# A seven-product output projection: where the first weight sums are formed, which raw weights are kept, and the order of sums in the feed-forward's second round

## The chip, the cores and the metric

The kernel runs on one core of a Trainium2 chip. The metric is the device time in microseconds (us): the median of three runs, and beside it one profiled execution, in which every instruction has a start, a duration and the line of the kernel that issued it.

The engines have the names of the profile: PE (TensorE, matmuls), PEld (its weight loads), DVE (VectorE), ACT (ScalarE), POOL (GpSimd) and SP (SyncE, which here only issues loads). Each engine runs its instructions in the order in which the compiler put them.

## The reference

One decoder layer over x of 512 rows and 1024 columns, all in float32: three gated branches, an output projection `w_o`, and a SwiGLU feed-forward.

```python
merged = g[:, :, 0] * y_a + g[:, :, 1] * y_b + g[:, :, 2] * y_c
x = x + merged @ w_o[l]

hf = rms_norm(x, ffn_norm_g[l]) @ w_ffn_in[l]
gt, up = jnp.split(hf, 2, axis=-1)
x = x + (jax.nn.silu(gt) * up) @ w_ffn_out[l]
```

`y_a` is an attention branch, `y_b` a convolution branch with a layer norm (it is the last one computed), `y_c` a short convolution.

## The kernel before

**Numbers.** Each float32 operand is split in two: `hi` is a rounded copy (fp32r, made by ScalarE, line 81), `lo` the rest (`src - hi`, by VectorE, line 82). A product of two operands is three matmuls: hi·hi, hi·lo, lo·hi (`mm3`, line 90 issues every matmul).

**Seven products.** `merged @ w_o` and the two halves of the second feed-forward matrix (12 and 10 row blocks, `ffn_out`) are done by Strassen's scheme in Winograd's form. The contraction goes over *pairs* of row blocks of 128: four pairs in `w_o`, six and five in the feed-forward halves. For a pair, the activations are cut in four quarters (`quarters`, lines 559 to 562 form four sums of quarters, then everything is split), and so is the weight: b11, b12, b21, b22, each 128 rows by 512 columns. The seven products 1 to 7 use, on the weight's side, b11, b21, b22, t2 - b21 (product 4), t1 = b12 - b11 (product 5), t2 = b22 - b12 + b11 (product 6) and t3 = b22 - b12 (product 7). In the feed-forward the operand of product 4 is formed afresh as t4. `seventh` does one product of one pair: two banks of PSUM, three matmuls each, six matmuls.

**Three rounds of the output projection.** Eight banks do not hold all results at once, so the products are done in rounds over the pairs:

- Round one: products 1, 6, 7 of all pairs. For each pair j, `raw3` loads b11, b12, b22 in three loads of 256 KB into one "raw" buffer; lines 811 and 812 form t3 and t2; `parts` splits b11 and `parts2` splits t2 and t3, both into "wh" and "wl" buffers. PE's order is (pair, product): (0,1), (1,1), (0,6), (0,7), (2,1), (1,6), (1,7), (3,1), (2,6), (2,7), (3,6), (3,7).
- `middle` (lines 614 to 623) joins the three results: copies by ScalarE, line 615 adds, line 620 makes the start value of product 4's banks (the returned `change`), and line 623 adds to two blocks of x1.
- Round two: products 2 and 4 of each pair. Line 827 loads all four b21 in one load of 1 MB; line 830 subtracts it from t2. Then lines 836 and 838 add to x1 (the last of these is `half`).
- Round three: products 5 and 3. `raw3` loads b11, b12, b22 once more for each pair, line 845 forms t1, `parts2` splits b22 and t1. PE's order is (0,5), (0,3), (1,5), a turn, (1,3), a turn, (2,5), (3,5), a turn, (2,3), a turn, (3,3). A turn (line 773) transposes a block of the finished x1 for the feed-forward; lines 777 and 778 scale and split it, line 783 squares it.

**Feed-forward.** `ffn_in` computes the two input products; `ffn_out` does round one (1, 6, 7) and then a round with 2, 3, 5 and 4: for pair j, `parts` splits b21 and b22 (from the raw weights), lines 934 to 936 form t1 and t4 in a "tt" buffer, and `parts` splits these. PE does (j,2), (j,3), then (j-1,5), (j-1,4). In the last half the last two pairs are regrouped, product by product.

**What sets the order.** PE's order is the program's own (a manual schedule). On the other engines a scheduler orders the instructions at compile time: by program order, with `tc.high_priority()` moving work ahead, `tc.issue_after(i)` keeping work behind instruction i, and each instruction waiting until its buffer is free. Buffers have tags, each with a fixed count: "raw" 3 (a load's target), "wh" and "wl" 3 (split weights), "t" 6 (temporaries, `tmp()`), "c" 4, "u" 16 (the normalised input of the branches, and later that of the feed-forward), "tt" 2, "l2" 1.

**Around it.** The branches are a queue of units, each one block of 128 output columns. The last branch has 16: a gate unit (24 matmuls) and a product unit (12) for each of eight blocks. Its last product unit ends with lines 650 and 651 and the last `quarters`. `drain()` empties the queue, and the output projection's code comes after it.

Of the kernel before, what the change touches and what calls it, by code (L numbers as in the profile page):

```python
# [9 lines left out]
F32R = mybir.dt.float32r  # L10
# [4 lines left out]
P = 128  # L15
S = 512
D = 1024
KT = D // P
# [17 lines left out]
def hybrid_layer(ctx, tc, x, mix_norm_g, w_in, q_norm_g, k_norm_g, w_attn_out, conf_dw_w,  # L36
# [23 lines left out]
    def alloc(tag, shape=(P, S), dt=F32):  # L60
        count[0] += 1
        where = ps if tag in ("mm", "z", "o") else odd if tag in ("c", "cf") else sb
        return where.tile(list(shape), dt, tag=tag, name=f"{tag}_{count[0]}", bufs=BUFS[tag])

    def psum(tag="mm"):
        return alloc(tag)

    def tmp(dt=F32, shape=(P, S)):
        return alloc("t", shape, dt)
# [533 lines left out]
    def x1_at(i, c):  # L603
        return x1[c][:, i, :]

    def middle(p1, p6, p7):


        p5 = [psum(tag) for tag in ("z", "o")]
        s2, s7 = [tmp(), tmp()], []  # L610
        with tc.high_priority(offset=PRIO):
            for i in range(2):
                s1 = tmp()
                nc.scalar.copy(s1, p1[i])
                nc.vector.tensor_add(s2[i], p6[i], s1)
                nc.scalar.copy(p5[i], s2[i])
            for i in range(2):
                s7.append(tmp())
                nc.scalar.copy(s7[i], p7[i])
                change = nc.vector.scalar_tensor_tensor(p7[i], p7[i], -1.0, s2[i], ALU.mult,  # L620
                                                        ALU.subtract)
        for i in range(2):
            nc.vector.tensor_add(x1_at(i + 2, 1), s7[i], x1_at(i + 2, 1))
        return p5, change.ins


    merged = {}
# [127 lines left out]

    bra = list(branch(0, w_attn_out, lambda: oT))
    queue += bra[:8] + [call(conf_mean_start)] + bra[8:]
    queue += branch(1, w_conf_out, lambda: hb, last=True)
    drain()


# [24 lines left out]
        return square  # L786

    n = KT // 2
    wo_q = lambda j, k, c: w_o[(2 * j + k) * P:(2 * j + k + 1) * P, c * S:(c + 1) * S]

    def raw3(j):
        with tc.high_priority():
            w = alloc("raw", (P, 3, S))
            for i, (k, c) in enumerate(((0, 0), (0, 1), (1, 1))):
                nc.sync.dma_start(w[:, i], wo_q(j, k, c))
        return [w[:, i] for i in range(3)]

    p1, p6, p7 = [[psum(tag) for _ in range(2)] for tag in ("mm", "mm", "z")]
    def after(*ins):
        stack = ExitStack()  # L800
        stack.enter_context(tc.high_priority())
        for i in ins:
            stack.enter_context(tc.issue_after(i))
        return stack

    t2s, last_sum, todo = [], [], []
    for j in range(n):
        b11, b12, b22 = raw3(j)
        with after(*last_sum):
            t3, t2 = tmp(), alloc("c")  # L810
            nc.vector.tensor_sub(t3, b22, b12)  # L811
            last_sum = [nc.vector.tensor_add(t2, t3, b11).ins]
        t2s.append(t2)
        one, = parts(b11.rearrange("p (n f) -> p n f", n=1))
        two = parts2(t2, t3)

        todo += [(j, 1, one, p1), (j, 6, two[0], p6), (j, 7, two[1], p7)]
        order = [0] if j == 0 else [2, 0, 1] if j < n - 1 else [2, 0, 1, 3, 4]
        for k in order:
            i, p, w, banks = todo[k]  # L820
            seventh(mT[i][p], w, banks, i == 0)
        todo = todo[1:] if j == 0 else todo[3:]
    p5, change = middle(p1, p6, p7)

    with tc.high_priority():
        b21 = alloc("raw", (P, n, S))
        nc.sync.dma_start(b21, w_o[:, :S].rearrange("(j k p) f -> p j k f", p=P, k=2)[:, :, 1])
    for j in range(n):
        with after(*[change][:j]):
            nc.vector.tensor_sub(t2s[j], t2s[j], b21[:, j])  # L830
        two, four = parts2(b21[:, j], t2s[j])
        seventh(mT[j][2], two, p1, False)
        seventh(mT[j][4], four, p7, False)
    with tc.high_priority(offset=PRIO):
# [4 lines left out]
    p3 = [psum("mm") for _ in range(2)]  # L839
    held = []  # L840
    for j in range(n):
        b11, b12, b22 = raw3(j)
        with after(*[half][:j]):
            t1 = tmp()
            nc.vector.tensor_sub(t1, b12, b11)
        held.append(parts2(b22, t1))
        if j == n - 2:
            continue
        for p in (5, 3):
            for i in range(j, j + 1) if j < n - 2 else (n - 2, n - 1):  # L850
                seventh(mT[i][p], held[i][p // 4], p5 if p == 5 else p3, i == 0 and p == 3)

                if j == 1 or j == n - 1 and (i, p) in ((n - 1, 5), (n - 2, 3)):
                    turn(len(u2))()
# [46 lines left out]
    def ffn_out(j0, h, last):  # L901
        n = len(h)
        rows_of = lambda j, k: w_ffn_out[(j0 + 2 * j + k) * P:(j0 + 2 * j + k + 1) * P]


        p1, p6, p7 = [[psum(tag) for _ in range(2)] for tag in ("mm", "mm", "z")]
        for j in range(n):
            with tc.high_priority():
                w = alloc("raw", (P, 3, S))
                nc.sync.dma_start(w[:, 0:2], rows_of(j, 0).rearrange("p (n f) -> p n f", n=2))  # L910
                nc.sync.dma_start(w[:, 2], rows_of(j, 1)[:, S:])
            b11, b12, b22 = [w[:, i] for i in range(3)]

            def t32(t3, t2):
                nc.vector.tensor_sub(t3, b22, b12)
                nc.vector.tensor_add(t2, t3, b11)

            one, = parts(w[:, 0:1])
            t3, t2 = parts(sums(t32))
            for p, w, banks in ((1, one, p1), (6, t2, p6), (7, t3, p7)):  # L920
                seventh(h[j][p], w, banks, j == 0)
        p5, change = middle(p1, p6, p7)
        p3, p4 = [psum("mm") for _ in range(2)], p7
        products = lambda j, p, w, banks, start: seventh(h[j][p], w, banks, start and j == 0)
        todo, behind, formed = [], [], []
        for j in range(n):
            with tc.high_priority():
                w = alloc("raw", (P, 2, 2, S))
                nc.sync.dma_start(w, w_ffn_out[(j0 + 2 * j) * P:(j0 + 2 * j + 2) * P].rearrange(
                    "(k p) (n f) -> p k n f", p=P, n=2))  # L930
            (b11, b12), (b21, b22) = [[w[:, k, i] for i in range(2)] for k in range(2)]

            def t14(t1, t4):
                nc.vector.tensor_sub(t1, b12, b11)  # L934
                nc.vector.tensor_sub(t4, b22, b21)  # L935
                formed[:] = [nc.vector.tensor_sub(t4, t4, t1)]  # L936

            tag = "u" if last and j == n - 1 else None  # L940
            two, three = parts(w[:, 1], tag)
            t1, t4 = parts(sums(t14, *behind, *(last_low if j > 1 and not tag else ())), tag)
            behind = [formed.pop().ins if j else change]
            todo.append([(j, 2, two, p1, False), (j, 3, three, p3, True),
                         (j, 5, t1, p5, False), (j, 4, t4, p4, False)])
            if last and j >= n - 2:
                now = [at[2:] for at in todo[:-1]] if j == n - 2 else [
                    [at[k] for at in todo[-2:]] for k in (2, 1, 3, 0)]
            else:
                now = [todo[-1][:2]] + [at[2:] for at in todo[:-1]]  # L950
                if j == n - 1:
                    now.append(todo[-1][2:])
            for group in now:
                for args in group:
                    products(*args)
            todo = todo[-1:] if not last or j < n - 2 else todo[-2:]

        def add(i, c, p, final, op=nc.vector.tensor_add):
            op(x1_at(i, c), x1_at(i, c), p)
            if last and final:  # L960
                nc.scalar.dma_start(out[i * P:(i + 1) * P, c * S:(c + 1) * S], x1_at(i, c))

        def add1():
            for i in range(2):
                add(i, 0, p1[i], True)

        def add3():
            for i in range(2):
                add(i, 1, p3[i], last)

        def add4():
            for i in range(2):
                add(i + 2, 0, p4[i], True, nc.vector.tensor_sub)

        def add5():
            for i in range(2):
                add(i + 2, 1, p5[i], True)
                add(i, 1, p5[i], False)

        for fn in (add5, add3, add4, add1) if last else (add1, add3, add5, add4):  # L980
            fn()
# [45 lines left out]
```

## Time and profile before

| | us |
|---|---|
| runs | 853.95, 854.52, 854.15 |
| median | 854.15 |
| profiled execution | 854.32 |
| its span (first to last instruction) | 852.6 |

The span is the part of the profiled execution in which the profile shows instructions; the rest lies around it. The profile names engine, line and operation, then the buffer written and those read, their shapes, and the count. "idle before" is the time for which the engine stood still before an instruction, and the name behind the arrow is what ended the wait. PE's durations are modelled and overlap; the distance from one start to the next is the rate. DVE's durations overlap too, by less than a tenth of a microsecond.

### The profile page before, as it was taken

How to read it: one execution, taken by the hardware profiler on the slowest of the kernel's cores; microseconds unless marked ns; L12 is line 12 of the kernel's file. 1: busy time of each engine (PE TensorE's matmuls, PEld its weight loads, DVE VectorE, ACT ScalarE, POOL GpSimd, SP SyncE). 2: the span in 40 equal slices, each digit the busy share in tenths (PEclk: the TensorE clock that was granted, in tenths of full speed). 3: DMA queues.
4: the chain of work that ended last, by engine and by line, in shares of the span. 5: the costliest groups of instructions: out<-in, count | busy, mean ns of one | idle time of the engine just before them, and what ended most of it. 6: DMA issues, size and time to landing. Idle time of an engine off the chain costs nothing.

```text
span 852.6 us, 9799 instructions
## 1 busy us (share of the span) xinstructions
PE 823.7 (97%) x3703; PEld 679.8 (80%) x3703; DVE 636.8 (75%) x952; ACT 411.5 (48%) x621; POOL 36.7 (4%) x60
## 2 busy tenths in 40 slices
PE   6999999999999999999979799999999999999997
PEld 5888887888888888888857578888888788888875
DVE  5598699896999999765667666555678775556786
ACT  5346698886663232654435355333345333333451
POOL 3100010111100000000000040000000000000000
PEclk9999999999999999999989899999999999999999
DMA  7333114122113233232324543222135542222452
GB/s 248 103 99 107 42 50 148 50 83 67 50 50 99 100 99 99 99 100 98 117 103 151 180 134 98 92 90 97 67 133 198 197 148 99 100 86 75 138 182 100
DMA packets 73148, 93.27 MB, mean 109 GB/s; under 512 B 2256, under 2 KB 56716, under 8 KB 73100
## 3 DMA queue, kind: packets, MB, share of 16 engines
q1 hardware_dynamic: 71932, 90.54, 31.9%
q10 hardware_dynamic: 1168, 2.10, 0.6%
q8 instruction: 29, 0.48, 0.2%
q14 instruction: 19, 0.16, 0.1%
HBM read 90.54 MB, written 2.10 MB: 109 GB/s over the span
## 4 chain that ended last, share of the span: by engine, by line
PE 87%; DVE 8%; ACT 2%; issue 2%; DMA 1%; SPq 0%; DVEq 0%; ACTq 0%
PE mm L90 74%; PE z L90 9%; PE o L90 3%; DVE wl L82 2%; ACT wh L81 1%; DMA m<-in_x_dram 1%; DVE cf L503 0%; DVE tt L935 0%; DVE z L620 0%; DVE tt L934 0%; DVE tt L936 0%; PE mm L773 0%; DVE u L778 0%; DVE t L811 0%; DVE t L284 0%
## 5 line engine op out<-in xcount | busy, mean ns | idle before, releaser
L90 PE MATMUL mm<-u,wh 128*128 128x512 f32 x1536 | 475.1, 390 | 0.1
L90 PEld LDWEIGHTS mm<-u,wh 128*128 128x128 f32 x1536 | 287.2, 188 | 59.7 <-DVE u L304 0.6
L90 PE MATMUL mm<-u,wl 128*128 128x512 f32 x768 | 299.2, 390 | 0.0
L81 ACT CAST wh<-raw 128x1024 fp32r<-128x1024 f32 (+1 forms) x157 | 145.2, 925 | 241.2 <-PE mm L90 192.3
L82 DVE TENSOR_TENSOR wl<-raw,wh 128x1024 fp32r<-128x1024 f32 (+1 forms) x155 | 165.8, 1070 | 39.7 <-ACT wh L81 39.2
L90 PEld LDWEIGHTS mm<-u,wl 128*128 128x128 f32 x768 | 144.2, 188 | 30.0
L503 DVE SCALAR_TENSOR_TENSOR cf<-cf,cols_w,cf 128x512 f32<-128x512 f32 x120 | 89.9, 749 | 3.7 <-ACT cf L501 1.2
L888 DVE TENSOR_TENSOR t<-mm,cf 128x512 f32<-128x512 f32 x22 | 15.2, 691 | 59.6 <-PE mm L90 59.6
L81 ACT CAST wh<-tt 128x1024 fp32r<-128x1024 f32 x21 | 22.1, 1054 | 38.4 <-DVE tt L936 26.7
L90 PE MATMUL mm<-m,wh 128*128 128x512 f32 x128 | 39.4, 389 | 0.0
L886 DVE TENSOR_TENSOR t<-mm,cf 128x512 f32<-128x512 f32 x22 | 15.1, 688 | 25.4 <-PE mm L90 25.4
L90 PE MATMUL mm<-wh,m 128*128 128x512 f32 x92 | 31.8, 401 | 0.0
L82 DVE TENSOR_TENSOR wl<-tt,wh 128x1024 fp32r<-128x1024 f32 x21 | 25.7, 1223 | 7.3 <-ACT wh L81 7.3
L90 PE MATMUL z<-wh,m 128*128 128x512 f32 x76 | 27.6, 396 | 0.8 <-DVE z L620 0.8
L90 PEld LDWEIGHTS mm<-m,wh 128*128 128x128 f32 x128 | 24.0, 188 | 4.9
L78 ACT ACTIVATE s<-s 128x384 f32<-128x384 f32 (+1 forms) x48 | 26.9, 561 | 1.1
L650 DVE TENSOR_TENSOR t<-mm,t 128x512 f32<-128x512 f32 x16 | 10.9, 689 | 19.6 <-PE mm L90 19.6
L90 PE MATMUL mm<-m,wl 128*128 128x512 f32 x64 | 24.9, 389 | 0.0
L785 POOL TENSOR_TENSOR cf<-cf,t 128x512 f32<-128x512 f32 x7 | 11.5, 1647 | 268.1 <-ACT t L783 267.9
L449 DVE SCALAR_TENSOR_TENSOR s<-z,s 128x384 f32<-128x384 f32 (+1 forms) x24 | 14.4, 599 | 11.6 <-ACT s L78 10.5
L90 PE MATMUL mm<-wh,s 128*128 128x512 f32 x48 | 17.8, 413 | 4.6 <-ACT wh L81 4.6
L81 ACT CAST m<-t 128x512 fp32r<-128x512 f32 x21 | 13.1, 624 | 17.7 <-DVE t L560 11.3
(286 smaller groups left out, 1142.0 us busy)
## 6 DMA issues: line engine op xcount, KB each, us to landing
raw<-in_w_in_dram SPq DMA_DIRECT2D x23, 1024.0 KB
raw<-in_w_ffn_in_dram SPq DMA_DIRECT2D x22, 1024.0 KB
raw<-in_w_ffn_out_dram SPq DMA_DIRECT2D x11, 1024.0 KB
raw<-in_w_o_dram SPq DMA_DIRECT2D x24, 256.0 KB
raw<-in_w_ffn_out_dram SPq DMA_DIRECT2D x11, 512.0 KB
raw<-in_w_in_dram SPq DMA_DIRECT2D x10, 512.0 KB
raw<-in_w_ffn_out_dram SPq DMA_DIRECT2D x11, 256.0 KB
m<-in_x_dram SPq DMA_DIRECT2D x8, 256.0 KB
```

The source lines that it names most:

```text
L78: table(nc.scalar.activation(o, i, f, **kw))
L81: (copy or nc.scalar.copy)(hi, src)
L82: return (sub or nc.vector.tensor_sub)(lo, src, hi.bitcast(F32))
L90: nc.tensor.matmul(o, lhsT, rhs, start=start, stop=stop, skip_group_check=True)
L449: marks.append(nc.vector.scalar_tensor_tensor(t, z, 0.0, t, ALU.max, ALU.add))
L503: nc.vector.scalar_tensor_tensor(y, pad[:, n:n + S], w(n), y, ALU.mult, ALU.add)
L650: nc.vector.tensor_mul(s[0], y, s[0])
L785: nc.gpsimd.tensor_add(sumsq, sumsq, s)
L886: nc.vector.tensor_mul(g, pg[0], rstd[0])
L888: nc.vector.tensor_mul(u, pu, rstd[0])
```

## The change

It has three parts.

1. **First weight sums.** A new function `first_sums(j)` does the loads of b11, b12, b22 and lines 811 and 812 for pair j. For pair 0 it is called from the queue of the last branch, after 13 of its 16 units, and it also splits b11, t2 and t3 there, into "tt", "tt" and "l2" instead of "wh" and "wl". For pairs 1 to 3 it is called where the code stood before. PE's order is unchanged.
2. **Raw weights held.** `wo_raw` keeps b11, b12, b22 of each pair up to round three, which loads nothing. Pairs 0 to 2 stay in the three "raw" buffers, the three pieces of pair 3 in "u" buffers, and b21 comes as four loads of 256 KB into "u" buffers. t1 of round three is taken from "c" instead of "t".
3. **A pair apart.** `middle` no longer does line 623 but returns it as `rest`, which is called in round three after pair 1's operands, and in the feed-forward after the third pass of the loop. In the feed-forward's second round the sums t1, t4 of pair j-1 are formed and split after the raw split of pair j; they are kept behind `change` alone, no longer behind the sums before and the raw split before. PE's order is unchanged.

```diff
-        for i in range(2):
-            nc.vector.tensor_add(x1_at(i + 2, 1), s7[i], x1_at(i + 2, 1))
-        return p5, change.ins
+        def rest():
+            for i in range(2):
+                nc.vector.tensor_add(x1_at(i + 2, 1), s7[i], x1_at(i + 2, 1))
+        return p5, change.ins, rest
...
-    queue += branch(1, w_conf_out, lambda: hb, last=True)
...
+    def wo_piece(j, k, c):
+        with tc.high_priority():
+            t = alloc("u")
+            nc.sync.dma_start(t, wo_q(j, k, c))
+        return t
...
+    def first_sums(j):
+        if j < n - 1:
+            with tc.high_priority():
+                w = alloc("raw", (P, 3, S))
+                for i, (k, c) in enumerate(((0, 0), (0, 1), (1, 1))):
+                    nc.sync.dma_start(w[:, i], wo_q(j, k, c))
+            wo_raw[j] = [w[:, i] for i in range(3)]
+        else:
+            wo_raw[j] = [wo_piece(j, k, c) for k, c in ((0, 0), (0, 1), (1, 1))]
+        b11, b12, b22 = wo_raw[j]
+        with after(*last_sum):
+            t3, t2 = tmp(), alloc("c")
+            nc.vector.tensor_sub(t3, b22, b12)
+            last_sum[:] = [nc.vector.tensor_add(t2, t3, b11).ins]
+        t2s.append(t2)
+        if j:
+            wo_parts[j] = lambda: (parts(b11.rearrange("p (n f) -> p n f", n=1))[0],
+                                   *parts2(t2, t3))
+            return
+        o = []
+        for src, tag in ((b11, "tt"), (t2, "tt"), (t3, "l2")):
+            with tc.high_priority():
+                w = alloc(tag, (P, 2, S), F32R)
+                split_to(w[:, 0], w[:, 1], src)
+            o.append((w[:, 0], w[:, 1]))
+        wo_parts[0] = lambda: o
+
+    units = list(branch(1, w_conf_out, lambda: hb, last=True))
+    queue += units[:13] + [call(lambda: first_sums(0))] + units[13:]
...
     for j in range(n):
-        b11, b12, b22 = raw3(j)
...
+        if j:
+            first_sums(j)
+        one, t2, t3 = wo_parts[j]()
...
-    with tc.high_priority():
-        b21 = alloc("raw", (P, n, S))
-        nc.sync.dma_start(b21, w_o[:, :S].rearrange("(j k p) f -> p j k f", p=P, k=2)[:, :, 1])
+    p5, change, rest = middle(p1, p6, p7)
+
+    b21 = [wo_piece(j, 1, 0) for j in range(n)]
...
-        b11, b12, b22 = raw3(j)
+        b11, b12, b22 = wo_raw[j]
         with after(*[half][:j]):
-            t1 = tmp()
+            t1 = alloc("c")
             nc.vector.tensor_sub(t1, b12, b11)
         held.append(parts2(b22, t1))
+        if j == 1:
+            rest()
```

In `ffn_out` the loop over the pairs becomes:

```diff
+        ends = n - 2 if last else n
+        pieces, ws = [], []
+        for j in range(n + 1):
+            if j < n:
+                with tc.high_priority():
+                    w = alloc("raw", (P, 2, 2, S))
+                    nc.sync.dma_start(w, w_ffn_out[(j0 + 2 * j) * P:(j0 + 2 * j + 2) * P].rearrange(
+                        "(k p) (n f) -> p k n f", p=P, n=2))
+                pieces.append(w)
+                two, three = parts(w[:, 1], "u" if last and j == n - 1 else None)
+                ws.append({2: two, 3: three})
+            if j:
+                (b11, b12), (b21, b22) = [[pieces[j - 1][:, k, i] for i in range(2)]
+                                          for k in range(2)]
+                t1, t4 = parts(sums(t14, *[change][:j - 1]), "u" if last and j == n else None)
+                ws[j - 1].update({5: t1, 4: t4})
+            if j == 2:
+                rest()
```

More of the change, by code (lines that the diff above doesn't have):

```diff
@@ L757, in hybrid_layer, with after @@
     queue += bra[:8] + [call(conf_mean_start)] + bra[8:]
-    queue += branch(1, w_conf_out, lambda: hb, last=True)
+    n = KT // 2
+    wo_q = lambda j, k, c: w_o[(2 * j + k) * P:(2 * j + k + 1) * P, c * S:(c + 1) * S]
+    wo_raw, t2s, last_sum, wo_parts = {}, [], [], {}
+    def wo_piece(j, k, c):
[3 more added lines that the diff above has]
+        return t
+    def after(*ins):
+        stack = ExitStack()
+        stack.enter_context(tc.high_priority())
+        for i in ins:
+            stack.enter_context(tc.issue_after(i))
+        return stack
+    def first_sums(j):
[26 more added lines that the diff above has]
+    queue += units[:13] + [call(lambda: first_sums(0))] + units[13:]
     drain()
@@ L788, in hybrid_layer @@
     n = KT // 2
-    wo_q = lambda j, k, c: w_o[(2 * j + k) * P:(2 * j + k + 1) * P, c * S:(c + 1) * S]
-    def raw3(j):
-        with tc.high_priority():
[L793 to L796, printed above, removed]
-    p1, p6, p7 = [[psum(tag) for _ in range(2)] for tag in ("mm", "mm", "z")]
[L799 to L806, printed above, removed]
-    for j in range(n):
-        b11, b12, b22 = raw3(j)
[L809 to L817, printed above, removed]
+    p1, p6, p7 = [[psum(tag) for _ in range(2)] for tag in ("mm", "mm", "z")]
+    todo = []
+    for j in range(n):
+        if j:
+            first_sums(j)
+        one, t2, t3 = wo_parts[j]()
+        todo += [(j, 1, one, p1), (j, 6, t2, p6), (j, 7, t3, p7)]
         order = [0] if j == 0 else [2, 0, 1] if j < n - 1 else [2, 0, 1, 3, 4]
@@ L822, in hybrid_layer @@
         todo = todo[1:] if j == 0 else todo[3:]
-    p5, change = middle(p1, p6, p7)
-    with tc.high_priority():
-        b21 = alloc("raw", (P, n, S))
-        nc.sync.dma_start(b21, w_o[:, :S].rearrange("(j k p) f -> p j k f", p=P, k=2)[:, :, 1])
+    p5, change, rest = middle(p1, p6, p7)
+    b21 = [wo_piece(j, 1, 0) for j in range(n)]
     for j in range(n):
         with after(*[change][:j]):
-            nc.vector.tensor_sub(t2s[j], t2s[j], b21[:, j])
-        two, four = parts2(b21[:, j], t2s[j])
+            nc.vector.tensor_sub(t2s[j], t2s[j], b21[j])
+        two, four = parts2(b21[j], t2s[j])
         seventh(mT[j][2], two, p1, False)
@@ L921, in ffn_out @@
                 seventh(h[j][p], w, banks, j == 0)
-        p5, change = middle(p1, p6, p7)
+        p5, change, rest = middle(p1, p6, p7)
         p3, p4 = [psum("mm") for _ in range(2)], p7
[L924 to L956, printed above, removed]
@@ new lines, in t14 @@
+        def t14(t1, t4):
+            nc.vector.tensor_sub(t1, b12, b11)
+            nc.vector.tensor_sub(t4, b22, b21)
+            nc.vector.tensor_sub(t4, t4, t1)
+        ends = n - 2 if last else n
[16 more added lines that the diff above has]
+                rest()
+            now = [(j, p) for p in (2, 3) if j < ends] + [(j - 1, p) for p in (5, 4)
+                                                          if 0 < j <= ends]
+            if last and j == n:
+                now = [(i, p) for p in (5, 3, 4, 2) for i in (n - 2, n - 1)]
+            for i, p in now:
+                seventh(h[i][p], ws[i][p], {2: p1, 3: p3, 4: p4, 5: p5}[p], p == 3 and i == 0)
```

## The prediction, made before the changed kernel ran

> **What bounds the kernel now.** I read the page first, for the bound of the whole. Then the busy time by stretch (columns: us, then busy time and count of PE, PEld, DVE, ACT and POOL, granted clock, DMA share, GB/s), for the stages that the change touches.
>
> ```profile
> span 852.6 us, 9799 instructions
> PE 823.7 (97%) x3703; PEld 679.8 (80%) x3703; DVE 636.8 (75%) x952; ACT 411.5 (48%) x621; POOL 36.7 (4%) x60
> ```
>
> ```profile
> 436.60:440.10 3.50, 1.52 (x7) 0.94 (x5) 3.17 (x7) 0.93 (x2) 0.00 (x0) 1.00 0.00 0
> 440.20:450.30 10.10, 6.14 (x14) 4.47 (x15) 9.87 (x18) 4.76 (x9) 0.00 (x0) 0.50 0.55 190
> ...
> 436.60:462.30 25.70, 19.66 (x73) 15.33 (x72) 20.88 (x36) 11.70 (x22) 0.00 (x0) 0.80 0.50 174
> 462.30:474.60 12.30, 11.47 (x50) 8.81 (x49) 11.05 (x20) 6.13 (x12) 0.00 (x0) 1.00 0.35 109
> ...
> 484.60:491.20 6.60, 4.32 (x9) 3.10 (x10) 3.54 (x5) 1.82 (x3) 1.62 (x1) 0.50 0.71 240
> ...
> 474.60:495.60 21.00, 15.55 (x65) 11.68 (x63) 13.58 (x20) 8.78 (x14) 1.62 (x1) 0.84 0.49 162
> ```
>
> PE is the bound at 97%, so only time in which PE waits or runs at a low clock can be won. The three rounds of the output projection are 436.6 to 462.3 (products 1, 6, 7), 462.3 to 474.6 (2, 4) and 474.6 to 495.6 (5, 3). The reader is to see the granted clock of 0.50 in two stretches of them, and a PE that is busy for 19.66 and 15.55 us of 25.70 and 21.00. Two smaller waits of PE there, from the view of waits:
>
> ```profile
> PE z L90 <- DVE z L620: 0.8, 1, 0.8
> ...
> PE mm L773 <- DVE v L859: 0.6, 1, 0.6
> ```
>
> PE's own rate comes from the chain of work: twelve matmuls that wait for nothing.
>
> ```profile
> 634.11 2.72 PE mm L90 x12
> ```
>
> That is 0.2267 us for one, and 1.36 us for a product of six. Round one has 12 products: 16.3 us of work in 25.7. Round three has 8, 10.9 us, and four turns of x1 (four transposes; 479.15 to 479.50 below, 0.35 us): 12.3 us of work in 21.0. So 9.4 and 8.7 us are lost.
>
> **Round one: the first sums inside the branch.** In order of time on VectorE (DVE), ScalarE (ACT) and PE:
>
> ```profile
> 436.87 0.69 DVE L650 TENSOR_TENSOR t<-mm,t 128x512 f32<-128x512 f32 x1 [6.27 <-PE mm L90]
> ...
> 438.32 0.43 DVE L559 TENSOR_TENSOR t<-v 128x256 f32<-128x256 f32 x1
> ...
> 439.33 0.42 DVE L561 TENSOR_TENSOR t<-v 128x256 f32<-128x256 f32 x1
> 439.67 0.68 DVE L811 TENSOR_TENSOR t<-raw 128x512 f32<-128x512 f32 x1
> ...
> 441.20 0.69 DVE L811 TENSOR_TENSOR t<-raw 128x512 f32<-128x512 f32 x1
> ...
> 444.21 0.69 DVE L82 TENSOR_TENSOR wl<-raw,wh 128x512 fp32r<-128x512 f32 x1
> ```
>
> ```profile
> 428.45 0.62 ACT L81 CAST wh<-raw 128x512 fp32r<-128x512 f32 x1 [1.50 <-issue]
> ...
> 440.44 0.62 ACT L81 CAST wh<-t 128x512 fp32r<-128x512 f32 x1 [1.36 <-DVE t L811]
> ...
> 442.00 0.62 ACT L81 CAST wh<-raw 128x512 fp32r<-128x512 f32 x1
> ```
>
> ```profile
> 437.73 0.39 PE L90 MATMUL mm<-wh,s 128*128 128x512 f32 x1
> 442.67 0.79 PE L90 MATMUL mm<-wh,s 128*128 128x512 f32 x1 [4.55 <-ACT wh L81]
> 444.95 0.80 PE L90 MATMUL mm<-wl,s 128*128 128x512 f32 x1 [1.49 <-DVE wl L82]
> ```
>
> PE's order is written by hand: (pair, product) (0,1), (1,1), (0,6), (0,7), (2,1) and so on. (0,1) ends with the matmul of 437.73; (1,1) waits for pair 1's raw weights, split at 442.00 and 444.21, though they were loaded long before (issued from 423.13, below). VectorE stands idle for 6.27 us before 436.87 with pair 0 loaded since the issue at 406.81. Both fit one reading, which is mine: buffers of one tag go out in program order. The first sum (L811, a "t") waits until the last quarters have taken their two "t" (L559, L561); pair 1's "wh" waits behind pair 0's second "wh", which needs that sum.
>
> ```profile
> 406.81 1.30 SPq L795 DMA_DIRECT2D raw<-in_w_o_dram  x3
> ...
> 423.13 19.50 SPq L795 DMA_DIRECT2D raw<-in_w_o_dram  x9
> 444.93 0.38 SPq L827 DMA_DIRECT2D raw<-in_w_o_dram  x1
> ```
>
> The change calls pair 0's sums before the last quarters ask, and gives its splits "tt" and "l2". These 2 sums and 3 splits cost 5 x 0.69 = 3.5 us of VectorE at most and 3 x 0.62 = 1.9 of ScalarE, under the cover of the 6.27 idle us; without it they would fall on the last split of the branch. Pair 1's raw split then takes the free "wh" that pair 0's took at 428.45. So (0,1), (1,1), (0,6), (0,7) run through from 436.60, to 442.0. What is late next is (2,1): pair 2's raw split stands behind pair 1's sums as pair 1's stood behind pair 0's. I move the pattern up by one pair, at the same times: its matmuls at 442.67 and 444.95. After these, 72 - 25 = 47 matmuls are left, 10.7 us: the round ends at 455.6 instead of 462.3, a gain of **6.7**. Bounds: 9.4 if (2,1) doesn't wait, 3.2 if the clock also drops (rival 1). I take 6.7, as its rows stand here.
>
> The Trainium skill ("TensorE: Matmul & The Clock Gate", Part 1) says that the clock is halved after an idle window of about 3.4 us that runs freely. By this rule the two new idle pieces (0.7 and 1.5 to 1.9 us) keep the clock. The trace is stricter: the clock is 1.00 up to 440.1 and 0.50 from 440.2, about 2 us after the matmul of 437.73, in a stretch of 3.50 us with PE busy for 1.52. By the rule the sum stays as it is; by the stricter reading rival 1 has its chance.
>
> **Loads.** The second round's one load (444.93) becomes four quarters in "u", the fourth pair's three pieces go to "u" too, and the third round's 12 loads (of 24 of 256 KB) are gone from SP's queue. The "u" come free with the last gate unit, which ends before 434, while round two starts after 455: cost nothing, by 20 us of cover.
>
> **Round two.** Same products, same order. The wait of 0.8 for L620 stays, and moving the two L623 (2 x 0.69) out of it may shorten it: bounds 0 to 0.8, I take **0**, since L623 stands behind L620 already.
>
> **Round three.**
>
> ```profile
> 484.00 0.75 DVE L778 SCALAR_TENSOR_TENSOR u<-mm,cols,u 128x512 fp32r<-128x512 f32 x1
> 484.66 1.28 DVE L845 TENSOR_TENSOR t<-raw 128x512 f32<-128x512 f32 x2
> ```
>
> ```profile
> 479.15 0.60 PE L773 MATMUL mm<-identr,v 128*128 128x128 f32 x4
> 479.50 0.48 PE L90 MATMUL mm<-wh,b 128*128 128x512 f32 x1
> ...
> 486.05 0.80 PE L90 MATMUL z<-wh,b 128*128 128x512 f32 x1 [4.47 <-ACT wh L81]
> 487.68 0.80 PE L90 MATMUL z<-wl,b 128*128 128x512 f32 x1 [0.83 <-DVE wl L82]
> ```
>
> PE waits 4.47 and 0.83 us for t1 of pairs 2 and 3 (L845 x2), formed only at 484.66; their "t" stand in program order behind the square of the second turn, which needs that turn's L778 (484.00). The change takes t1 from "c", whose four buffers the second round gives back, and the raw weights are there. Then only the adds that end with `half` precede them, as they precede pair 1's today: (2,5), at 7 us into the round, finds them split. With that goes the 0.50 clock. PE then needs 12.3 + 0.5 for the wait at (1,5), which I keep, = 12.8. VectorE has 13.58 + 2 x 0.69 (the L623 that move in) = 15.0, of which one 1024-wide split for the feed-forward (1.22, below) may come after the round: 13.8. The larger counts: 21.0 - 13.8 = **7.2**. Bounds 8.7 (nothing kept) and 3.5 (VectorE's 15.0 and a third of its 7.4 idle us of today: 17.5). The wait of 0.6 for L859 stays.
>
> **Feed-forward, second round.** PE's order is the same; what moves is that pair j's t1 and t4 come behind pair j+1's raw split.
>
> ```profile
> 662.79 1.22 DVE L82 TENSOR_TENSOR wl<-raw,wh 128x1024 fp32r<-128x1024 f32 x1
> ```
>
> ```profile
> 664.06 0.50 PE L90 MATMUL mm<-wl,m 128*128 128x512 f32 x1 [0.79 <-DVE wl L82]
> ```
>
> ```profile
> 827.50 0.50 PE L90 MATMUL mm<-wl,m 128*128 128x512 f32 x1 [0.83 <-DVE wl L82]
> ...
> 836.52 0.49 PE L90 MATMUL z<-wh,b 128*128 128x512 f32 x1 [0.78 <-ACT wh L81]
> 837.78 0.50 PE L90 MATMUL z<-wl,b 128*128 128x512 f32 x1 [0.77 <-DVE wl L82]
> ```
>
> ```profile
> 835.42 1.05 ACT L81 CAST wh<-tt 128x1024 fp32r<-128x1024 f32 x1 [3.46 <-DVE tt L936]
> ```
>
> From 836.52 to 837.78 is 1.26 us for a wait of 0.77, where 0.23 would be due: such a wait costs 1.0. In the first half PE waits once, for a raw split, which the change puts first: **1.0** (bounds 0 and 1.0). In the second half it waits three times: 3.1. The new order of "wh" is the order in which PE uses them, but near the end two splits of 1.05 + 1.22 us each get their buffer only one pair of products (2.72) before PE asks: 0.4 us of room, on a VectorE that has hardly a pause there. I keep 0.9 of the 3.1: **2.2**, bounds 3.1 and -2.4 (today's waits, and both hand-overs late by one split of 1.22).
>
> **Sum.** 6.7 + 7.2 + 1.0 + 2.2 = 17.1 us. The profiled execution took 854.32 (span 852.6 and 1.7 around it), 0.17 above the median of 854.15; against the median 854.15 - 17.1 = 837.05, **837.0 us**.
>
> **Rivals.**
> 1. *The clock drops again in round one* (for: the stretch of 3.50 above, and up to 2.6 idle us between 442.0 and 444.95; against: a matmul stands between them). At 0.50 the 12 matmuls from 444.95 to 450.30 took 0.45 us each instead of 0.23; 8 to 16 such are 1.8 to 3.5 more: 839.6. Chance 0.17.
> 2. *VectorE becomes the bound of round three* (for: its 15.0 us of work; against: some of it can come later). Gain 3.5 instead of 7.2: 840.7. Chance 0.15.
> 3. *The feed-forward end gains nothing, its hand-overs come late*: -2.4 instead of 2.2: 841.6. Chance 0.11.
> 4. *The change doesn't do what it says*: pair 0's sums still land behind the last product, as the scheduler orders them at compile time. Round one gains 0: 843.7. Chance 0.07.
> 5. *Slower: the prefetch is lost.* All three "raw" buffers are held into round three, so no load of the feed-forward's input weights can start before they come free. If they come free only at the round's end, three loads stand in a row, 3 x 4.9 us (rows below), plus a split of 1.05 + 1.22 and the low clock, 3.5: 837.0 + 20.5 = 857.5. It decides from a release some 17 us later than I work out, with the loads late by more than the sum above: pair 0's buffer is free when its two operands are split, before round three begins, and the load has 13 us. Chance 0.05.
>
> SP's row and the landing for the 4.9:
>
> ```profile
> 803.31 19.80 SPq L929 DMA_DIRECT2D raw<-in_w_ffn_out_dram  x5
> ```
>
> ```profile
> 827.63 1.14 ACT L81 CAST u<-raw 128x512 fp32r<-128x512 f32 x2 [1.63 <-DMA raw<-in_w_ffn_out_dram]
> ```
>
> The last of those five issues ends at 823.1 and so begins at 822.7 (0.38 for one, as the row of 444.93 has it); ScalarE waits for the landing until 827.63.
>
> **How the numbers follow.** The forecast has 0.45. Its own range is 834.3 (round one without its wait) to 839 (small misses). One at a time, the ends of the terms and rivals 1 to 4 reach from 834.3 to 843.7; I add 1.3 on each side for two of them at once: 833.0 to 845.0. It leaves out rival 5 and larger sums of misses. A measurement of this kernel can tell 0.2% (1.7 us) from no change: faster 0.93, same 0.02, slower 0.05.
>
> **What would show it.** Granted clock 1.00 through round one and three; L811 for pair 0 before 436; PE's waits in round one 2.7 us or less, and at (2,1); the third round's t1 right behind the adds of `half`; no wait near 664. Reads from HBM fall by 12 x 0.25 MB. Wrong if PE waits in the last branch, at the first feed-forward weights, or at the end of the second half.

## The result, and the profile after

| | before | after |
|---|---|---|
| runs, us | 853.95 to 854.52 (four) | 839.71, 839.83, 841.86, 840.57 |
| median, us | 854.33 | 840.20 |
| ratio of the means, 95% interval | | 0.9839 [0.9822, 0.9856] |
| profiled execution, us | 854.32 | 839.71 |

The change saves 14.1 us in the medians; 17.1 were forecast. The page of the changed kernel begins:

```profile
span 838.0 us, 9783 instructions
...
PE 818.6 (98%) x3703; PEld 677.9 (81%) x3703; DVE 635.0 (76%) x952; ACT 410.9 (49%) x621; POOL 36.2 (4%) x60
```

PE is still the bound, with the same 3703 matmuls. The busy time by stretch, for the stages that the change touches (columns as in the prediction: us, then busy time and count of PE, PEld, DVE, ACT and POOL, granted clock, DMA share, GB/s):

```profile
435.60:456.40 20.80, 18.33 (x73) 14.50 (x73) 18.21 (x32) 10.10 (x19) 0.00 (x0) 0.92 0.20 69
...
456.40:468.70 12.30, 11.46 (x49) 8.79 (x49) 10.43 (x19) 6.10 (x12) 0.00 (x0) 1.00 0.21 68
468.70:482.90 14.20, 13.04 (x65) 10.31 (x63) 12.21 (x20) 8.54 (x14) 1.29 (x1) 1.00 0.49 164
482.90:488.70 5.80, 4.92 (x28) 3.87 (x28) 4.32 (x6) 3.02 (x5) 3.70 (x2) 1.00 0.27 84
642.20:674.80 32.60, 32.60 (x146) 26.99 (x144) 29.35 (x39) 13.63 (x15) 0.00 (x0) 1.00 0.54 193
804.00:833.80 29.80, 27.93 (x121) 22.17 (x119) 25.28 (x37) 9.46 (x13) 0.00 (x0) 1.00 0.32 121
```

Round three (468.70) now runs at a clock of 1.00 throughout, and the first half's second round (642.20) has PE busy for all of its 32.60 us. Round one (435.60) still has a mean clock of 0.92. Taken from the start of the first matmul of each stage to that of the next (for the last half, to the start of its last matmul):

| stage | before, us | after, us | change | forecast |
|---|---|---|---|---|
| round one | 25.77 | 20.81 | -4.96 | -6.7 |
| round two | 12.25 | 12.27 | 0.02 | 0 |
| round three | 21.02 | 14.23 | -6.79 | -7.2 |
| its end to the fifth turn of x1 | 2.84 | 3.80 | +0.96 | 0 |
| the fifth to the eighth turn | 2.50 | 2.01 | -0.49 | 0 |
| feed-forward, first half, second round | 34.19 | 32.64 | -1.55 | -1.0 |
| feed-forward, last half, second round | 30.55 | 29.75 | -0.80 | -2.2 |
| sum | | | -13.61 | -17.1 |

The stages between these agree within 0.02 us. Round one also starts 0.96 us earlier (435.64 against 436.60), but that is no gain of the change: most of it arises in the first 20 us of the program, and in the other profiles below round one starts anywhere from 435.93 to 436.80. The 13.6 of the stages and this 0.96 make up the 14.6 by which the two profiled executions differ; the medians lie 14.1 apart.

**Round one, row by row.** VectorE, ScalarE and PE of the changed kernel in order of time:

```profile
425.38 0.68 DVE L791 TENSOR_TENSOR t<-raw 128x512 f32<-128x512 f32 x1
...
438.91 0.68 DVE L791 TENSOR_TENSOR t<-raw 128x512 f32<-128x512 f32 x1
...
443.46 0.68 DVE L82 TENSOR_TENSOR wl<-raw,wh 128x512 fp32r<-128x512 f32 x1
```

```profile
441.25 0.61 ACT L81 CAST wh<-raw 128x512 fp32r<-128x512 f32 x1
```

```profile
435.64 1.52 PE L90 MATMUL mm<-tt,s 128*128 128x512 f32 x6
...
439.72 1.52 PE L90 MATMUL z<-l,m 128*128 128x512 f32 x6
441.92 0.49 PE L90 MATMUL mm<-wh,s 128*128 128x512 f32 x1 [0.68 <-ACT wh L81]
444.20 0.79 PE L90 MATMUL mm<-wl,s 128*128 128x512 f32 x1 [1.79 <-DVE wl L82]
```

Pair 0's first sum (L791) starts at 425.38, ten us before the round, and PE takes its operands from "tt" and "l" without a pause. The first wait comes at (2,1), for pair 2's raw split (441.25 on ScalarE, 443.46 on VectorE).

One thing the prediction had not foreseen. On VectorE round two's subtraction of b21 for pair 0 (L856) now stands ahead of the last product's sums in the branch (L651 and after):

```profile
435.51 0.69 DVE L856 TENSOR_TENSOR c<-c,u 128x512 f32<-128x512 f32 x1 [5.24 <-DMA u<-in_w_o_dram]
```

It waits for the late load of b21. Most of that wait costs nothing, since L651 needs PE's last product anyway; but L651 starts 0.48 us after the first matmul of round one instead of 0.27 in the kernel before. Where the load landed earlier against the round (runs 6, 7 and 8 below) it starts at 0.27 again, and the first wait of PE is 0.48 instead of 0.68.

### The profile page after: what moved, and what is told of

The parts are those of the page before. It is cut to its first block, busy times and chain, and to the rows that moved or that the text cites. A ratio compares the mean times of both kernels' runs of the same rounds, so it can differ in the third digit from the quotient of the medians.

```text
span 838.0 us, 9783 instructions
## 1 busy us (share of the span) xinstructions
PE 818.6 (98%) x3703; PEld 677.9 (81%) x3703; DVE 635.0 (76%) x952; ACT 410.9 (49%) x621; POOL 36.2 (4%) x60
## 3 DMA queue, kind: packets, MB, share of 16 engines
HBM read 87.39 MB, written 2.10 MB: 107 GB/s over the span
## 4 chain that ended last, share of the span: by engine, by line
PE 89%; DVE 7%; issue 2%; ACT 1%; DMA 1%; SPq 0%; DVEq 0%; ACTq 0%
PE mm L90 75%; PE z L90 10%; PE o L90 3%; DVE wl L82 2%; DMA u<-in_w_o_dram 1%; ACT wh L81 1%; PE mm L297 1%; DVE cf L503 0%; DMA m<-in_x_dram 0%; PE z L297 0%; PE mm L822 0%; DVE tt L955 0%; DVE tt L956 0%; DVE tt L954 0%; DVE t L791 0%
## 5 line engine op out<-in xcount | busy, mean ns | idle before, releaser
L81 ACT CAST wh<-raw 128x1024 fp32r<-128x1024 f32 (+1 forms) x150 | 140.5, 937 | 240.5 <-PE mm L90 194.4
L82 DVE TENSOR_TENSOR wl<-raw,wh 128x1024 fp32r<-128x1024 f32 (+1 forms) x148 | 161.0, 1088 | 37.6 <-ACT wh L81 36.9
L90 PE MATMUL mm<-wh,m 128*128 128x512 f32 x88 | 29.6, 392 | 0.0
L78 ACT ACTIVATE t<-t 128x512 f32<-128x512 f32 x31 | 19.6, 631 | 3.7 <-DVE t L914 3.6
L90 PEld LDWEIGHTS mm<-wh,m 128*128 128x128 f32 x88 | 16.8, 191 | 3.6
```

Of the source, the lines that this page charges most:

```text
L78: table(nc.scalar.activation(o, i, f, **kw))
L81: (copy or nc.scalar.copy)(hi, src)
L82: return (sub or nc.vector.tensor_sub)(lo, src, hi.bitcast(F32))
L90: nc.tensor.matmul(o, lhsT, rhs, start=start, stop=stop, skip_group_check=True)
```

## The experiments

Each run is compared with the kernel before on the same chip. Runs 1 to 4, 5 to 8, and 9 and 10 ran on three chips, where the kernel before took 853.62, 853.75 and 853.85 us in the median, against 854.33 beside the changed kernel; so a difference of half a microsecond between medians from different groups says little. Stages are those of the table above. The expectations count the turns of x1 from 0, so that their fourth turn is the fifth here. Theory, from the prediction: buffers of one tag go out in program order, so an operand that PE wants next stands behind work of which it needs nothing.

**1. The changed kernel, with t1 of round three from "t" again.**

```diff
-            t1 = alloc("c")
+            t1 = tmp()
```

> The changed kernel with one line undone: t1 of round three is a "t" buffer again; the raw weights stay held. Theory (the order in which buffers of one tag are given out caused round three's wait): the sums of pairs 2 and 3 stand behind the second turn's square again, PE waits some 4.5 + 0.8 us, the clock falls to 0.50, and round three takes 20 to 21 us instead of 14.2: about 846.7 in all. Rival (the loads that are gone made the gain): round three stays at 14.2 and the time at 840.2.

847.89 us in the median (846.25 to 848.71), ratio 0.9926 [0.9911, 0.9941]. Round three took 20.96 us, and the old waits are back. PE's timeline of this run:

```profile
480.61 0.80 PE L90 MATMUL z<-wh,b 128*128 128x512 f32 x1 [3.87 <-ACT wh L81]
482.25 0.79 PE L90 MATMUL z<-wl,b 128*128 128x512 f32 x1 [0.84 <-DVE wl L82]
```

One word of the diff holds the whole gain of round three. The raw weights were still held here, and nothing was loaded in the round: that alone gives nothing.

**2. The kernel before, with only that word changed.**

```diff
-            t1 = tmp()
+            t1 = alloc("c")
```

> The kernel before with that one line alone: t1 of round three from "c", all loads of round three made again. Theory (tag order): round three falls from 21.0 to 14 or 15 us, with no low clock in it, 847.5 to 848.5 in all. Rival (held weights): it stays at 21.0 and 854.3.

847.59 us, ratio 0.993 [0.9913, 0.9946]; round three 14.24 us, as after the whole change (14.23), with its twelve loads still in place. The end of the round went from 2.84 to 3.80 us, as after the change too: this loss comes with the gain. One wait of PE is left in the round, the same as in the changed kernel:

```profile
478.75 0.50 PE L90 MATMUL z<-wl,m 128*128 128x512 f32 x1 [1.16 <-DVE wl L82]
```

**3. The kernel before, with only pair 0's first sums and splits in the last branch.** The loads and sums of pair 0 move as in the change; pairs 1 to 3, the raw weights of round three, the tag of t1 and the feed-forward stay as they were.

```diff
+    queue += units[:13] + [call(first_sums)] + units[13:]
...
     for j in range(n):
+        if j:
...
+        else:
+            one, two = pair0[0], pair0[1:]
```

> The kernel before with the first sums of pair 0 inside the last branch, and nothing else of the change. Theory: round one goes from 25.8 to 20.8 us (19.0 if the clock holds), the rest stays: 849.3, or 847.5. Rival (round one also needs the fourth pair's loads in their own buffers): round one stays above 23 us, over 851.5.

848.03 us, ratio 0.9931 [0.9916, 0.9946]; round one 20.73 us, round three 21.17. PE waits 0.48 and 1.78 us at (2,1), and the clock falls at 445.20 as in the changed kernel. Round one is this edit's alone.

**4. The kernel before, with only the feed-forward part.** `rest` is called at once in the output projection.

```diff
+    p5, change, rest = middle(p1, p6, p7)
+    rest()
```

> The kernel before with the feed-forward's second round a pair apart, and nothing else. Theory (the three parts add up): its rounds two go from 34.2 to 32.6 and from 30.55 to 29.75 us, 852.0 in all. Rival (the gain there comes from work that the output projection no longer pushes ahead): 854.3.

The two stages took 32.64 and 29.77 us, as in the changed kernel: 2.3 us less than before. The median of ten runs fell by 0.6 only, from 853.6 to 853.0, ratio 0.9987 [0.9978, 0.9997]; the profiled execution, 851.67, was among the fastest of the ten. In that profile round three, which this edit doesn't touch, took 22.17 us instead of 21.02. PE's timeline and the busy time by stretch:

```profile
484.62 0.50 PE L90 MATMUL z<-wh,b 128*128 128x512 f32 x1 [4.47 <-ACT wh L81]
486.25 0.80 PE L90 MATMUL z<-wl,b 128*128 128x512 f32 x1 [1.13 <-DVE wl L82]
```

```profile
485.60:492.20 6.60, 5.95 (x16) 4.83 (x17) 3.17 (x5) 0.00 (x0) 0.05 (x1) 0.50 0.88 310
```

The first wait is that of before (4.47). But the slow clock begins 0.9 us after the wait's end, not 1.5 us ahead of it as before (484.50 against 486.05), so more of its 6.83 us falls on matmuls: 5.95 us of PE in these 6.60, where before had 4.32. So the place of the slow stretch moves this round by about a microsecond. It can also move the other way: round one took 25.02 us in this profile instead of 25.77, with a slow stretch of 6.83 us instead of 10.24.

For the executions without a profile there is the mean granted clock of each run. It is 0.9900 in the mean of these ten and 0.9912 in that of the thirteen runs of the kernel before, which over 852 us is about 1.0 us of full clock. At an equal clock the gain shows: at 0.992 the two runs with the edit took 851.26 and 851.67, the six of the kernel before 853.28 to 853.71; at 0.990 the means lie 1.3 us apart (six runs against two). So a lower clock hid part of the gain in these ten runs. Why it was lower isn't shown.

**5. The changed kernel, with pair 2's raw split asked for ahead of pair 1's sums.** This aims at the wait at (2,1).

```diff
+        if j == 1:
+            one_of(1)
+            load(2)
+            one_of(2)
         one, t2, t3 = wo_parts[j]()
```

`one_of(j)` makes the split of pair j's b11 once.

> The changed kernel with the split of pair 2's b11 asked for before pair 1's sums are split (it takes the buffer that these took). Theory (in round one PE waits at (2,1) because that split stands behind pair 1's in the order of the "wh" buffers, and the low clock follows from this wait): the waits of 0.7 and 1.8 us and the 3.4 us at 0.50 go, a wait of about 1 us at (1,6) may come, round one takes 16.4 to 17.5 us instead of 20.8, 836.2 to 837.3 in all. Rival (VectorE is the bound of round one): the wait only moves to (1,6), round one stays above 19.5.

837.40 us (836.72 to 838.85), ratio 0.9815 [0.9799, 0.9831]. Round one took 17.85 us, 0.35 above the upper end of what was expected, and its clock stayed at 1.00. One wait is left, at the next pair's product, (1,6):

```profile
444.40 0.50 PE L90 MATMUL mm<-wl,m 128*128 128x512 f32 x1 [0.94 <-DVE wl L82]
```

**6. The changed kernel, with the last pair's sums kept behind those of the pair before.** In the last half of the changed kernel VectorE forms both pairs' t1 and t4 together (VectorE, ScalarE and PE in order of time):

```profile
818.85 0.68 DVE L954 TENSOR_TENSOR tt<-raw 128x512 f32<-128x512 f32 x1
819.45 0.68 DVE L955 TENSOR_TENSOR tt<-raw 128x512 f32<-128x512 f32 x1
820.05 1.28 DVE L956 TENSOR_TENSOR tt<-tt 128x512 f32<-128x512 f32 x2
```

```profile
820.84 1.05 ACT L81 CAST wh<-tt 128x1024 fp32r<-128x1024 f32 x1 [3.62 <-DVE tt L956]
```

```profile
818.38 0.50 PE L90 MATMUL z<-wl,m 128*128 128x512 f32 x1 [0.36 <-DVE wl L82]
...
821.94 0.50 PE L90 MATMUL z<-wh,b 128*128 128x512 f32 x1 [0.75 <-ACT wh L81]
823.20 0.50 PE L90 MATMUL z<-wl,b 128*128 128x512 f32 x1 [0.76 <-DVE wl L82]
```

L954 and L955 of 818.85 belong to the last pair; L956 of the pair before, which PE needs first, stands behind them, and ScalarE has waited 3.62 us for it.

```diff
-                t1, t4 = parts(sums(t14, *[change][:j - 1]), ...)
+                t1, t4 = parts(sums(t14, *([change][:j - 1] if j < n or not last else formed[-1:])), ...)
```

`formed` lists the L956 of each pair.

> The changed kernel with the last pair's sums kept behind those of the pair before, in the last half of the feed-forward. Theory (the two waits at (3,5) come from the order of VectorE, in which t4 of pair 3 stands behind work for pair 4): the waits of 0.75 and 0.76 us there fall to 0.3 or less, round two goes from 29.75 to about 28.3, 838.7 in all. Rival (as predicted, the late buffer of the split, one pair of products ahead): the waits stay, 840.2.

839.41 us, ratio 0.9837 [0.9821, 0.9854]. The stage took 29.03 us instead of 29.75; 28.3 were expected. Of PE's waits the one of 0.75 is gone; these are left in its timeline:

```profile
817.89 0.50 PE L90 MATMUL z<-wl,m 128*128 128x512 f32 x1 [0.39 <-DVE wl L82]
821.51 0.50 PE L90 MATMUL z<-wl,b 128*128 128x512 f32 x1 [0.57 <-DVE wl L82]
```

The changed kernel still lost 2.3 us here (the 3.1 of the prediction less 0.80), so the order on VectorE is a third of that, not all of it. In this run VectorE is busy for all 8.38 us from 813.13 to the end of the wait at 821.51, so what is left looks like the amount of VectorE's work; no run tried that. This run showed something else by chance: round one, with the waits of the changed kernel, took 19.15 us and kept its clock (see the last section).

**7. The changed kernel, with two 1024-wide splits for the feed-forward's first weights kept behind the last adds of round three.** VectorE and PE of the changed kernel at the end of the round:

```profile
482.43 1.22 DVE L82 TENSOR_TENSOR wl<-raw,wh 128x1024 fp32r<-128x1024 f32 x1
483.57 0.74 DVE L827 SCALAR_TENSOR_TENSOR u<-mm,cols,u 128x512 fp32r<-128x512 f32 x1
484.44 1.45 DVE L82 TENSOR_TENSOR wl<-raw,wh 128x1024 fp32r<-128x1024 f32 x1
485.82 1.27 DVE L887 TENSOR_TENSOR v<-v,mm 128x512 f32<-128x512 f32 x2
```

```profile
486.75 1.82 PE L822 MATMUL mm<-identr,v 128*128 128x128 f32 x12 [0.79 <-DVE v L887]
```

The fifth turn waits for L887, and two splits stand ahead of it.

```diff
     for i in range(2):
-        nc.vector.tensor_add(x1_at(i, 1), x1_at(i, 1), p3[i])
+        add3 = nc.vector.tensor_add(x1_at(i, 1), x1_at(i, 1), p3[i]).ins
+    for k in (2, 3):
+        queued_after[nsplit[0] + k] = [add3]
```

> The changed kernel with VectorE's part of the second and third feed-forward weight split kept behind the last two adds to x1. Theory (these splits stand ahead of the adds and hold up the last four turns): the time from round three's end to the fourth turn falls from 3.8 to about 2.8 us, 839.2 in all. Rival (PE needs these splits as early): PE waits for them right after the turns, 840.2.

A miss: 841.5 us, ratio 0.9856 [0.9841, 0.9872]; end to fifth turn 4.89 us. VectorE and PE in the order that came out:

```profile
483.29 1.39 DVE L887 TENSOR_TENSOR v<-v,mm 128x512 f32<-128x512 f32 x2
484.59 2.81 DVE L82 TENSOR_TENSOR wl<-raw,wh 128x1024 fp32r<-128x1024 f32 x2
487.33 0.74 DVE L827 SCALAR_TENSOR_TENSOR u<-mm,cols,u 128x512 fp32r<-128x512 f32 x1
```

```profile
488.12 0.50 PE L90 MATMUL mm<-u,wh 128*128 128x512 f32 x1 [1.77 <-DVE u L827]
```

The adds came early, as meant, but the low split of the fourth turn (L827) fell behind both splits, and PE needed that one next.

**8. The changed kernel, with t1 of pair 1 no longer kept behind `half`.** VectorE at the start of round three of the changed kernel, and the one wait of PE there:

```profile
468.66 1.28 DVE L864 TENSOR_TENSOR v<-v,z 128x512 f32<-128x512 f32 x2
469.86 1.29 DVE L871 TENSOR_TENSOR c<-raw 128x512 f32<-128x512 f32 x2
471.06 0.68 DVE L871 TENSOR_TENSOR c<-u,u 128x512 f32<-128x512 f32 x1
471.66 0.68 DVE L82 TENSOR_TENSOR wl<-raw,wh 128x512 fp32r<-128x512 f32 x1
472.26 0.68 DVE L82 TENSOR_TENSOR wl<-c,wh 128x512 fp32r<-128x512 f32 x1
```

```profile
473.00 0.50 PE L90 MATMUL z<-wl,m 128*128 128x512 f32 x1 [1.16 <-DVE wl L82]
```

With the tag no longer in their way, all three remaining t1 (L871) are formed in a row as soon as `half` (L864) is done, and (1,5) waits for its split (472.26) behind them.

```diff
-        with after(*[half][:j]):
+        with after(*[half][:max(0, j - 1)]):
```

> The changed kernel with t1 of pair 1 no longer kept behind the adds to x1. Theory (the wait of 1.16 us at (1,5) comes from three sums in a row ahead of its split): it goes, round three falls from 14.2 to about 13.0, 839.0 in all. Rival (VectorE has no room in round three): the wait moves on, 840.2.

Round three took 12.77 us, and PE doesn't wait in it at all. The median is 839.59, ratio 0.9837 [0.9819, 0.9854]: 0.6 below the changed kernel, with intervals that overlap, so the gain of 1.46 shows in the stage and not for certain in the time.

**9. The edits of 5, 6 and 8 together.**

> The changed kernel with three edits at once, each of which ran by itself before: pair 2's raw split in front of pair 1's (round one 20.81 to 17.85 us, clock held), the sums of the last pair behind those of the last but one (last half 29.75 to 29.03 us), and the t1 of pair 1 not held behind half (round three 14.23 to 12.77 us). If the terms are independent they add: 2.96 + 0.72 + 1.46 = 5.1 less, 835.1 us. Rival: in their medians the three gave only 2.8, 0.8 and 0.6 less than the changed kernel's 840.2 (837.40, 839.41, 839.59), 4.2 in all, 836.0 us. A third, that the end of round three takes back what its middle wins (the adds and the feed-forward's first splits being late by VectorE, not by PE): round three wins nothing, 836.5.

835.48 us (834.53 to 836.46), ratio 0.9784 [0.9771, 0.9798]. Round one took 17.68 us, round three 12.77, the last half 29.01: each what it was alone, and the end of round three 3.80, unchanged. So the third rival falls; the median lies between the 835.1 and 836.0 of the other two. The page of this run, and round one by stretch, now at a clock of 1.00:

```profile
span 833.6 us, 9785 instructions
```

```profile
436.00:453.70 17.70, 16.90 (x74) 13.38 (x73) 17.38 (x32) 9.53 (x18) 0.00 (x0) 1.00 0.26 92
```

VectorE is busy for 17.38 of these 17.70 us, and the one wait that PE has left there, 0.80 us at 444.66, is for its split: round one is now close to what VectorE can do from the time at which it starts (see run 10).

**10. The same, with the two splits behind the last adds and behind the fourth turn's low split.**

```diff
+    for k in (2, 3):
+        queued_after[nsplit[0] + k] = [add3, turned[3]]
```

`turned` lists the low split (L827 of the changed kernel) of each turn.

> As the run with three edits, and the two 1024-wide splits of the feed-forward's first weights kept behind both the last adds and the low split of the third turn (in the miss before, that low split stood behind the two splits, and PE waited 1.77 us for it). In the changed kernel the fourth turn waits 0.79 us for the last add and starts 3.80 us after the end of round three, where 2.84 passed in the kernel before. If the two splits ahead of the last adds are that wait: it goes, the fourth turn comes 0.8 to 1.0 us earlier, and the time is 0.8 to 1.0 below the run with three edits. Rival: the two splits are themselves late then (2.45 us of VectorE, for products that PE asks for next), the wait only moves, and the time is the same or up to 1 us above.

834.26 us (833.88 to 835.33), ratio 0.9772 [0.9759, 0.9785]. The fifth turn came 2.88 us after the round's end instead of 3.80, without a wait. VectorE's timeline of this run (L839 is L827 of the changed kernel, L903 its L887):

```profile
478.79 1.38 DVE L903 TENSOR_TENSOR v<-v,mm 128x512 f32<-128x512 f32 x2
480.10 0.74 DVE L839 SCALAR_TENSOR_TENSOR u<-mm,cols,u 128x512 fp32r<-128x512 f32 x1
480.76 3.44 DVE L82 TENSOR_TENSOR wl<-raw,wh 128x1024 fp32r<-128x1024 f32 x2
```

The fifth to the eighth turn took 0.35 less (1.66), and the next stage 0.39 more: PE waits 0.59 us there for a later low split, the rival in small. That is 0.9 us net in the stages and 1.2 in the medians, whose intervals overlap.

Round one, which this edit doesn't touch, took 18.18 us in this profile instead of 17.68 in that of run 9. The rows at its start, on VectorE:

```profile
436.10 0.69 DVE L872 TENSOR_TENSOR c<-c,u 128x512 f32<-128x512 f32 x1 [5.12 <-DMA u<-in_w_o_dram]
...
437.31 0.68 DVE L651 TENSOR_TENSOR t<-mm,t 128x512 f32<-128x512 f32 x1
```

L872 is L856 of the changed kernel. With it and a raw split ahead, L651 starts 0.97 us after the round's first matmul (436.34), where run 9 had 0.50 and run 5 0.65; the rounds took 18.18, 17.68 and 17.85. So in these three runs the landing of b21 moves the start of VectorE's work, and the round with it. Keeping that subtraction behind the branch's last sum was not tried.

This is the fastest version of the study, some 6 us below the changed kernel.

## Why the prediction came out as it did

The direction, the two places of the gain and their mechanism held; the time, 840.2, lies in the range and 3.2 above the forecast of 837.0. By its own steps:

- **Round one, forecast -6.7, measured -4.96.** The pattern "moved up by one pair" came as drawn: waits of 0.68 and 1.79 us at (2,1), where 0.7 and 1.5 to 1.9 were named. The step that failed is the price: the sum took the clock to hold, and rival 1 (given 0.17) happened. With the clock held (run 6) the round takes 19.15 us against the 19.0 of the sum (455.6 less 436.6); with the drop 20.81, and 20.73 and 20.76 in runs 7 and 8, which have the same waits as run 6. So 1.6 us of the miss is the clock, and the 0.17 was too small a chance: five of the six profiles with these waits lost it (last section). Run 5 settles that both hang on pair 2's raw split standing behind pair 1's sums.
- **Loads, "cost nothing, by 20 us of cover".** The cover was counted up to the start of round two, but VectorE takes pair 0's b21 already at the start of round one (L856, above). In the changed kernel this delayed VectorE by 0.2 us; in run 10, where VectorE bounds the round, the round took 0.5 us more than in run 9.
- **Round two, 0.** Measured 0.02.
- **Round three, forecast -7.2, measured -6.79.** The cause was right: runs 1 and 2 give and take the whole gain with the tag of t1. The size came near for a wrong reason. The sum let VectorE's 13.8 us bound the round. It did not: VectorE is busy for 12.21 of 14.20 us, and run 8 does the round in 12.77. The two adds of `rest` (L624), which the sum moved into the round, ran in round two, at 458.26 and 463.68. PE without a wait takes those 12.77 us, where the sum had 12.3; the rest is the wait at (1,5), taken as 0.5, measured as 1.16 and worth 1.46 by run 8, because the freed t1 of pairs 2 and 3 are formed ahead of pair 1's split.
- **"The wait of 0.6 for L859 stays": it grew.** It is L887 now and waits 0.79 us; with one more split ahead of it the end of the round and the turns after it lost 0.96 - 0.49 = 0.47 us. Run 2 shows the same loss with the tag alone, so it belongs to round three's gain, and the sum had no term for it.
- **Feed-forward, first half, forecast -1.0, measured -1.55.** The one wait is gone, as drawn; the bound set at 1.0 was too low: 1.1 of the gain lies at that wait, the rest at several smaller delays.
- **Feed-forward, last half, forecast -2.2, measured -0.80.** The loss that was kept back, 0.9, was put down to "wh" buffers handed over late. Two waits of 0.75 are left at the end of the second half, which the prediction had named as a sign of being wrong, and the rows shown with run 6 put the first on VectorE's order: with the sums kept behind `change` alone, the last pair's go ahead of the sum that PE needs first. The step mis-sized the rest (2.3 of the 3.1 stayed) and misnamed a part of its cause: the order accounts for 0.72, and what is behind the other 1.6 wasn't tried (in run 6 VectorE has no pause there).
- **The other rivals.** VectorE as bound of round three, the last half without any gain, sums that land late, and the lost prefetch did not happen. HBM reads fell from 90.54 to 87.39 MB, the twelve loads of 0.25 MB, without an effect on the time that the runs show.

Together: 1.74 + 0.41 + 0.47 + 1.40 - 0.55 + 0.02 = 3.5 us, the distance of 17.1 from 13.6.

## What to carry to other kernels

When a scheduler hands out buffers by tag in program order, look for a small temporary whose tag is shared with work that ends later; moving that one temporary to a free tag gave 6 to 7 us here, while the larger edit around it (weights held, loads removed) gave nothing that could be measured. Work that such a barrier had held back then runs as early as it can, also ahead of what the critical engine wants next, so look again at the order behind the barrier. Price any wait that leaves PE half idle or more for a few microseconds with a chance of the slow clock on top.

## What the runs showed of the hardware

**The clock changes on a grid that runs freely.** In each profile all changes of the granted clock lie apart by multiples of 3.413 us, whatever PE does in between: the slow stretches of the kernel before last 10.24 and 6.83 us, and in run 1 the clock falls at 446.12, 480.26 and 831.83, which is 34.14 and 351.57 apart, 10 and 103 times 3.413. Where the grid lies against the program differs from execution to execution. What seems to count is how busy PE is between two lines of this grid: the same waits cost the slow clock in one execution and not in another. The stretch of the grid that holds the wait at (2,1), and the one after it, in the changed kernel:

```profile
440.56:443.97 3.41, 1.18 (x5) 0.41 (x3) 3.41 (x6) 2.43 (x5) 0.00 (x0) 1.00 0.00 0
443.97:447.38 3.41, 3.18 (x8) 2.50 (x9) 2.32 (x5) 0.64 (x2) 0.00 (x0) 0.50 0.00 0
```

And the stretch of the grid in run 6 that holds most of the same wait, by the same view; this run kept the clock, and its grid is that of its two changes, at 10.98 and, behind the last matmul, 837.01:

```profile
441.08:444.49 3.41, 1.79 (x7) 0.93 (x5) 3.41 (x7) 2.84 (x6) 0.00 (x0) 1.00 0.00 0
```

With these waits in round one, five of six profiles lost the clock, at PE busy for 34 to 48% of the stretch (the changed kernel, runs 1, 3, 7 and 8), and the sixth kept it at 53%. Elsewhere it was lost once at 55% (run 1, last half, 1.6 us longer by it), and kept at 43% (run 4, round three; run 9, at its last matmuls), 45 and 48% (run 7, at its last matmuls and after round three) and 51% (run 8, at its last matmuls). In the twelve profiles of this study, a full clock was lost after every stretch of the grid with PE busy for 41% or less and after none with 56% or more; of the nine stretches from 43 to 55%, three lost it. So with modelled ends of matmuls no sharp threshold can be read.

The Trainium skill ("TensorE: Matmul & The Clock Gate", Part 1) gives an activity window of 4096 cycles, about 3.4 us, that runs freely: the grid of 3.413 us agrees. It gives the halved clock after at least one idle window; here the window before a fall was in ten cases not idle but 30 to 55% busy, and by the measurement a window like that is enough.
